# Gate weights of the first four experts in pages by row blocks, and one embedding piece in the seventh group

## The chip, the cores and the metric

The kernel runs on one core of a Trainium2 chip. The metric is the device time of one execution in microseconds (us); the times given are medians of several executions. Five engines work side by side: TensorE (PE; its weight loads are shown as PEld), VectorE (DVE), ScalarE (ACT), GpSimd (POOL) and SyncE (SP), which issues the transfers from the chip's memory (HBM). Sixteen DMA engines carry the transfers.

## The reference

One decoder layer over 256 tokens of width 1024, followed by a last RMSNorm. What is computed after the token mixer matters here:

```
h   = RMSNorm(x)
[z | xBC | dt | q | k | v | g_ssd | g_att] = h @ W_in
x   = x + (sigmoid(g_ssd) * SSD(...) @ W_ssd_out + sigmoid(g_att) * MoBA(...) @ W_att_out) @ W_o
x   = x + HierMoE(RMSNorm(x))            # 4 groups of 8 experts; top-1 group, top-2 experts in it
x   = x + sigmoid(RMSNorm(x) @ W_pg) * (p @ W_ple)
out = RMSNorm(x)
```

An expert has a gate and an up matrix of 1024 x 256 and a down matrix of 256 x 1024, float32: 1 MB each, so 96 MB for the 32 experts, all of which are read.

## The kernel before, in words

**The first part** (to about 285 us) is the input projection, the state-space mixer, the attention and the output projections. Each weight block is loaded, split into two parts by ACT and DVE (`w_split`), and multiplied on PE. The planner of the language orders the instructions of PE, ACT, DVE and POOL here by simulated costs; two stretches (`start`, `middle`) and the end (`ends`) are in the order in which they are written. SP's order is always the written one.

**Pages.** The pool `pgp` has 26 pages (NPAGE, line 45) of 8 KB in each of the 128 partitions. A 1 MB weight tile fills one. A page comes back when the last instruction that reads its tile is done; a load that needs a page waits for that on SP, and everything behind it on SP waits too. `prefetch(n)` (line 854) takes n entries from `queue` (line 846) and issues their loads. The entries are, for each group of four experts, four gate tiles, four up tiles, four down tiles. In the last group the up and down tiles are loaded in halves; before it stand the loads for the embedding (PLE_AT), and after it the four blocks of the last gate matrix (`pgr`). During the first part `prefetch` is called at fixed steps (PREFETCH, line 29); at the end of `middle` it is called until 25 entries have been issued (line 1193): both matrices of groups 0 and 1, their down tiles, and the first gate tile of group 2.

**The groups.** `quad(q)` (line 1278) does four experts: a gather of their tokens (`gather_quad`; group 0 is gathered in `middle`), the gate product, the up product (both into `pgu`, the loop over i at line 1286, over k at 1289 and over the four experts j at 1292), the weights of the combination (`combine_weights`), the activation (`hidden`), the down product (`down`, two halves n) and the scatter. After the gate product and after the up product the four tiles are dropped and up to four loads are issued (lines 1295 to 1297); after `down` four more (line 1309). In group 0 it is three and three, since two pages go to `hTg1` and `y_sb`.

**The embedding.** `embed()` (line 1398) is called before `quad(6)`. It spreads the last norm's weights, transposes p and returns `piece(t, c)` and `piece_out(t, c)`: two 128x512 products into one accumulator (PE), and its copy to SBUF on ACT. There are four pieces. `quad(7)` stands in the written order and calls two of them from `inside`, between the first and the second half of the up product; the third stands in `hidden`, and the fourth around `down(7, 0)`.

**The end** (lines 1555 to 1628): `down` of group 7, scatter, transposes, the last gate product (`ple_gate`, needs the `pgr` blocks), the last norm.

Accumulators: the tag `acc` has four PSUM banks, used in turn by gathers, downs, scatters and pieces.

Of the kernel before, what the change touches and what calls it, by code (L numbers as in the profile page):

```python
# [25 lines left out]
NK = D // P  # L26
# [12 lines left out]
EARLY_SPLITS = 5  # L39
SPLIT_FIRST = 260  # L40
PLE_AT = 72
EMBED_AT = 6
MAXOV = 16
EPS = 1e-6
NPAGE = 26
# [135 lines left out]
def emit(ctx, tc, nc, A, out):  # L181
    V, SC, PE, G, SP = nc.vector, nc.scalar, nc.tensor, nc.gpsimd, nc.sync
# [7 lines left out]
    def pg(shape, name, dt=F32):  # L190
        return pgp.tile([P] + shape, dt, tag="pg", name=name)

    def qt(shape, name, dt=F32):
        return qp.tile([P] + shape, dt, tag="qt", name=name)

    def acc(name, n=2):
        return [psp.tile([P, 512], F32, tag="acc", name=f"{name}_{i}", bufs=4) for i in range(n)]

    def ps1(shape, name, parts=P, dt=F32):
        return psp.tile([parts] + shape, dt, tag="s", name=name, bufs=2)  # L200
# [46 lines left out]
    def spread(row, ones, name):  # L247

        for c, o in enumerate(acc(name)):
            mm(o, ones, row[0:1, 512 * c:512 * c + 512], True, True)  # L250
            SC.copy(row[:, 512 * c:512 * c + 512], o)
# [554 lines left out]
        T["OT_hi"], T["OT_lo"] = OT_hi, OT_lo  # L806


    EW = {}
    PG_ORDER = [(0, 0), (0, 1), (1, 0), (1, 1)]  # L810
    pgraw, tail = [], {}
    nload = [0]
# [1 line left out]
    def expert_load(e, w):  # L814
        if w[0] == "d":
            if w != "d1":
                EW["d", e] = pg([4, 512], f"wd{e}")
            r = slice(2 * int(w[1]), 2 * int(w[1]) + 2) if w[1:] else slice(0, 4)
            SP.dma_start(EW["d", e][:, r], A["w_d"][e].rearrange("(p r) d -> p r d", r=4)[:, r])
        else:  # L820
            if w[1:] != "1":
                EW[w[0], e] = pg([NK, 256], f"w{w[0]}{e}")
            r = slice(4 * int(w[1]), 4 * int(w[1]) + 4) if w[1:] else slice(0, NK)
            SP.dma_start(EW[w[0], e][:, r], A["w_" + w[0]][e].rearrange("(p k) f -> p k f", k=NK)[:, r])

# [13 lines left out]
    def ple_gate_load(kh, c):  # L839
# [3 lines left out]
                             ap=[[2048, P], [1, 2048]]))  # L843
        pgraw.append(raw)

    queue = deque((expert_load, 4 * q + j, w) for q in range(NE // 4) for w in "gud" for j in range(4))
    for _ in range(8):
        queue.pop()
    queue.extend((expert_load, NE - 4 + j, w) for w in ("u0", "u1", "d0", "d1") for j in range(4))
# [4 lines left out]
    def prefetch(n):  # L854

        for _ in range(min(n, len(queue))):
            f, *a = queue.popleft()
            f(*a)
            nload[0] += 1
# [348 lines left out]
    def gather_quad(q):  # L1208
        if q == 1 or q % 2 == 0:
            hTg["page"] = pg([NK, 256], f"hTg{q}")  # L1210
        g, sel = hTg["page"][:, :, P * (q % 2):P * (q % 2) + P], new_sel(q)
        for t in range(NT):
            select(sel, q, t)
        gather(lambda a, b: g[:, a:b], lambda t: flat(sel, t), P, str(q), SC)
        hTg[q] = (lambda k: g[:, k]), sel
# [45 lines left out]
    def combine_weights(q, sel):  # L1261
        sq = qt([512], f"selw{q}")
        for t in range(NT):
            V.tensor_tensor(sq[:, t * P:(t + 1) * P].rearrange("p (e c) -> p e c", e=4), sel[:, t],
                            comb[:, t, 4 * q:4 * q + 4, None].to_broadcast([P, 4, CAP]), op=OP.mult)
        sw = weights_T(sq, sq[:, 256:512], P, str(q))
        return sw, factors(lambda t: flat(sel, t), P, str(q))

    def down(q, n, py, hT):
        for c in range(2):  # L1270
            for j in range(4):
                mm(py[n][32 * j:32 * j + 32, :], hT[:, c, 32 * j:32 * j + 32],
                   EW["d", 4 * q + j][:, 2 * n + c, :], c == 0, c == 1)
        if n:
            for j in range(4):
                EW.pop(("d", 4 * q + j))

    def quad(q, between=lambda: None, inside=lambda: None, wait=lambda: None):
        if q:
            gather_quad(q)  # L1280
        g, sel = hTg.pop(q)
        if q % 2:
            hTg.pop("page")
        es = range(4 * q, 4 * q + 4)
        pgu = ps1([512], f"gu{q}")
        for i, w in enumerate("gu"):
            if (q, i) == (7, 1):
                sw, f = combine_weights(q, sel)
            for k in range(NK):
                if (i, k) == (1, 4):  # L1290
                    inside()
                for j in range(4):
                    mm(pgu[32 * j:32 * j + 32, 256 * i:256 * i + 256], g(k)[:, 32 * j:32 * j + 32],
                       EW[w, 4 * q + j][:, k, :], k == 0, k == NK - 1)
            for j in range(4):
                EW.pop((w, 4 * q + j))
            prefetch(4 - (q == 0))
        if q == 0:
            hT0.clear()
        if q < 7:  # L1300
            sw, f = combine_weights(q, sel)
        g = None
        between()
        hT = hidden(pgu, f, P, str(q), wait=wait)
        if q == 7:
            return sw, hT
        py = acc(f"py{q}")
        down(q, 0, py, hT), down(q, 1, py, hT)
        prefetch(4)
        y = [qt([512], f"ye{q}{c}") for c in range(2)]  # L1310
        for c in range(2):
            (V.tensor_copy if c else SC.copy)(y[c], py[c])  # L1312
        scatter(sw, y, P, str(q))

    def load_rounds():
        return nc.values_load(nov_i, min_val=0, max_val=MAXOV - 1,
                              skip_runtime_bounds_check_because="512 choices fill at most 15 rounds beyond the first")
# [80 lines left out]
    def embed():  # L1398

        pin, wple, pT = tail["pin"], tail.pop("wple"), tail["pT"]  # L1400
        spread(tail["fnw"], pT[0:1, 0, 0:P], "fnw")
        ppt = ps2([2, S], "ppT")
        for k in range(2):
            for t in range(NT):
                PE.transpose(ppt[:, k, t * P:(t + 1) * P], pin[:, t, k * P:(k + 1) * P], ident)
        SC.copy(pT, ppt)
        pe = pe_[0] = pg([NT, D], "pemb")

        def piece(t, c, ks=(0, 1)):
            if (t, c) not in pps:  # L1410
                pps[t, c] = acc(f"pp{t}{c}", 1)[0]
            for k in ks:
                mm(pps[t, c], pT[:, k, t * P:(t + 1) * P], wple[:, k, half(c)], k == 0, k == 1)

        def piece_out(t, c):
            SC.activation(pe[:, t, half(c)], pps.pop((t, c)), AF.Copy, scale=0.5)

        return piece, piece_out

    for q in range(7):  # L1420
        if q == EMBED_AT:
            piece, piece_out = embed()
            nov = load_rounds()
        quad(q)
    while queue:
        prefetch(1)
    y_sb = ys[0]
# [120 lines left out]
                SC.activation(o, fin[t][:, 1, s], AF.Copy, scale=inv)  # L1548
            SP.dma_start(out[t * P:(t + 1) * P, s], o)

    def two_pieces():
        piece(0, 0), piece_out(0, 0)
        piece(0, 1), piece_out(0, 1)

    sw, hT = quad(7, other_rounds, two_pieces, lambda: piece(1, 0))
    piece_out(1, 0)
    py = acc("py7")
    y = [qt([512], f"ye7{c}") for c in range(2)]
# [5 lines left out]
    piece = None  # L1564
# [16 lines left out]
    hT = sw = y = py = None  # L1581
# [63 lines left out]
```

## Time and profile before

| | |
|---|---|
| median of 3 runs | 530.16 us (530.08 to 530.96) |
| profiled execution | 530.37 us, its span 528.6 us |
| PE busy | 495.0 us (94%) |
| DVE busy | 287.0 us (54%) |
| ACT busy | 212.8 us (40%) |
| DMA | 154.78 MB, 292 GB/s from HBM over the span |

The span is what the trace covers; 1.8 us of the execution lie outside it. A busy PE in this profile is one that has a matmul in it, also where that matmul runs at half clock. The busy share over the whole span mixes stages with different limits; which resource ends a stage last has to be read stage by stage.

### The profile page before, as it was taken

To read this page: it belongs to the slowest core of one execution; us is meant where nothing else is said; L and a number is where in the kernel's file an instruction comes from. 1 tells how busy PE (TensorE), PEld (TensorE's weight loads), DVE (VectorE), ACT (ScalarE), POOL (GpSimd) and SP (SyncE) were. 2 spreads that over 40 slices of the span, in tenths; PEclk is the share of its full clock that TensorE was granted. 3 is DMA by queue.
4 is the path that set the end of the run, shared out by engine and by line. 5 is a ranking of instruction groups with operands and counts; after the bars stand their busy time and mean duration, and the time that the engine had idled before them with its cause. 6 is when DMAs were issued, how large, how long until landed. Compare 5 with 4: busy or idle time off the path is not lost. (4 is left out here: it accounts for less than half of the span.)

```text
span 528.6 us, 9502 instructions
## 1 busy us (share of the span) xinstructions
PE 495.0 (94%) x3911; PEld 380.6 (72%) x3911; DVE 287.0 (54%) x585; ACT 212.8 (40%) x428; POOL 16.1 (3%) x22
## 2 busy tenths in 40 slices
PE   6999999999999999999999999898898989699993
PEld 3899887798889979899998855363554635254583
DVE  4899788886659497545585533033130312030675
ACT  5836759537456086544154321111101112012674
POOL 3000012000000000000000000000000000000001
PEclk9999999999999999999999999899989989899998
DMA  8990077365429204697969989999999999999802
GB/s 306 428 410 8 1 249 318 112 221 227 172 81 387 79 2 160 249 392 255 367 233 383 400 329 427 426 428 426 426 425 425 425 423 427 426 420 417 343 1 79
DMA packets 29842, 154.78 MB, mean 293 GB/s; under 512 B 4307, under 2 KB 9187, under 8 KB 14437
## 3 DMA queue, kind: packets, MB, share of 16 engines
q1 hardware_dynamic: 29796, 154.15, 72.4%
q8 instruction: 31, 0.51, 0.4%
q14 instruction: 15, 0.11, 0.1%
HBM read 153.08 MB, written 1.06 MB: 292 GB/s over the span
## 5 line engine op out<-in xcount | busy, mean ns | idle before, releaser
L293 DVE TENSOR_TENSOR wl<-wr,wh 128x1024 fp32r<-128x1024 f32 (+4 forms) x92 | 100.7, 1131 | 9.7 <-ACT wh L292 8.8
L292 ACT CAST wh<-wr 128x1024 fp32r<-128x1024 f32 (+4 forms) x92 | 82.6, 961 | 14.4 <-DMA wr<-in_w_ao 4.3
L208 PE MATMUL py<-wd,hq 128*32 128x512 f32 x256 | 39.2, 711 | 3.2 <-ACT hq L1237 3.2
L208 PE MATMUL ps_t<-wl,hT_hi 128*128 128x448 f32 (+2 forms) x112 | 39.9, 374 | 1.6 <-DVE wl L293 1.5
L208 PE MATMUL ps_t<-wh,hT_hi 128*128 128x448 f32 (+2 forms) x112 | 39.5, 375 | 0.0
L208 PE MATMUL ps_t<-wh,hT_lo 128*128 128x448 f32 (+2 forms) x112 | 39.1, 367 | 0.0
L1230 DVE SCALAR_TENSOR_TENSOR hq<-hq,gu 128x256 f32<-128x256 f32 x8 | 3.4, 421 | 61.7 <-ACT hq L1229 61.7
L208 PE MATMUL gu<-wu,hTg 128*32 128x256 f32 x512 | 32.8, 396 | 3.2 <-DMA wu<-in_w_u 3.2
L208 PE MATMUL gat<-sel,x_sb 128*128 128x128 f32 x256 | 30.4, 276 | 0.5 <-DVE ng L1066 0.5
L208 PEld LDWEIGHTS gat<-sel,x_sb 128*128 128x128 f32 x256 | 29.4, 192 | 1.8 <-issue 1.2
L208 PE MATMUL sca<-ye,selw 128*128 128x512 f32 x64 | 30.1, 611 | 0.1
L208 PE MATMUL gu<-wg,hTg 128*32 128x256 f32 x512 | 30.1, 381 | 0.0
L208 PEld LDWEIGHTS gu<-wu,hTg 128*32 128x32 f32 x512 | 17.5, 114 | 16.7 <-DMA wu<-in_w_u 4.2
L208 PEld LDWEIGHTS py<-wd,hq 128*32 128x32 f32 x256 | 10.4, 125 | 26.2 <-issue 18.8
L1312 DVE COPY ye<-py 128x512 f32<-128x512 f32 x7 | 4.8, 691 | 41.8 <-PE py L208 41.8
L208 PEld LDWEIGHTS ps_t<-wl,hT_hi 128*128 128x128 f32 x112 | 21.0, 191 | 5.1 <-DVE wl L293 3.6
L208 PEld LDWEIGHTS sca<-ye,selw 128*128 128x128 f32 x64 | 11.0, 189 | 18.0 <-issue 10.1
L208 PEld LDWEIGHTS ps_t<-wh,hT_lo 128*128 128x128 f32 x112 | 21.3, 190 | 1.8 <-DVE hT_lo L358 0.4
L208 PEld LDWEIGHTS gu<-wg,hTg 128*32 128x32 f32 x512 | 15.4, 110 | 9.9 <-issue 0.2
L1229 ACT ACTIVATE hq<-gu,f 128x256 f32<-128x256 f32 x8 | 3.8, 473 | 46.5 <-PE gu L208 45.0
L208 PEld LDWEIGHTS ps_t<-wh,hT_hi 128*128 128x128 f32 x112 | 21.2, 192 | 1.7
L1136 ACT ACTIVATE hTg<-gat,par 128x128 f32<-128x128 f32 x32 | 9.2, 368 | 28.2 <-PE gat L208 26.8
(310 smaller groups left out, 1095.3 us busy)
## 6 DMA issues: line engine op xcount, KB each, us to landing
wg<-in_w_g SPq DMA_DIRECT2D x32, 1024.0 KB, 13.3
wu<-in_w_u SPq DMA_DIRECT2D x28, 1024.0 KB, 15.9
wd<-in_w_d SPq DMA_DIRECT2D x28, 1024.0 KB, 19.4
wr<-in_w_in SPq DMA_DIRECT2D x16, 1024.0 KB, 5.4
wr<-in_w_in SPq DMA_DIRECT2D x10, 896.0 KB, 10.1
wr<-in_w_so SPq DMA_DIRECT2D x4, 1024.0 KB, 4.8
wr<-in_w_ao SPq DMA_DIRECT2D x4, 1024.0 KB, 7.1
wr<-in_w_o SPq DMA_DIRECT2D x4, 1024.0 KB, 6.8
```

Source lines behind the costliest of these rows:

```text
L208: mm = lambda o, l, r, start, stop: PE.matmul(o, l, r, start=start, stop=stop, skip_group_check=True)
L292: SC.copy(hi[:, s], raw[:, s])
L293: V.tensor_tensor(lo[:, s], raw[:, s], hi[:, s].bitcast(F32), op=OP.subtract)
L1136: SC.activation(dst(k + i, k + i + 1)[:, 0], o[:, i], AF.Copy, scale=R("mnw")[:, k + i:k + i + 1])
L1229: SC.activation(hd[0:n], pgu[:, 0:256], AF.Tanh, scale=f[0:n, 0:1])
L1230: V.scalar_tensor_tensor(hd[0:n], hd[0:n], 1.0, pgu[:, 0:256], op0=OP.add, op1=OP.mult)
L1312: (V.tensor_copy if c else SC.copy)(y[c], py[c])
```

## The change

The gate tiles of experts 0 to 3 are no longer one page for each expert. Page i (i = 0 to 3, `first_load`) holds the row blocks k = 2i and 2i + 1 of all four experts; it is filled by four transfers of 256 KB, one for each expert, with 2 KB for each partition. The gate product of group 0 reads those pages; after each odd k one page is dropped and one load is issued. After its up product two loads are issued instead of three. The count of entries and their order behind the first four are the same. The second edit: the first of the four embedding pieces is written behind `quad(6)` instead of inside `quad(7)`.

```
+    def first_load(i):
+
+        FW[i] = pg([4, 2, 256], f"wf{i}")
+        for j in range(4):
+            SP.dma_start(FW[i][:, j], A["w_g"][j].rearrange("(p k) f -> p k f", k=NK)[:, 2 * i:2 * i + 2])
+
     queue = deque((expert_load, 4 * q + j, w) for q in range(NE // 4) for w in "gud" for j in range(4))
+    for _ in range(4):
+        queue.popleft()
+    queue.extendleft((first_load, 3 - i) for i in range(4))
...
                     mm(pgu[32 * j:32 * j + 32, 256 * i:256 * i + 256], g(k)[:, 32 * j:32 * j + 32],
-                       EW[w, 4 * q + j][:, k, :], k == 0, k == NK - 1)
-            for j in range(4):
-                EW.pop((w, 4 * q + j))
-            prefetch(4 - (q == 0))
+                       FW[k // 2][:, j, k % 2] if (q, i) == (0, 0) else EW[w, 4 * q + j][:, k, :], k == 0, k == NK - 1)
+                if (q, i, k % 2) == (0, 0, 1):
+                    FW.pop(k // 2)
+                    prefetch(1)
+            if (q, i) != (0, 0):
+                for j in range(4):
+                    EW.pop((w, 4 * q + j))
+                prefetch(2 if q == 0 else 4)
...
-    for q in range(7):
-        if q == EMBED_AT:
-            piece, piece_out = embed()
-            nov = load_rounds()
+    for q in range(6):
         quad(q)
+    piece, piece_out = embed()
+    nov = load_rounds()
+    quad(6)
+    piece(0, 0), piece_out(0, 0)
...
-    def two_pieces():
-        piece(0, 0), piece_out(0, 0)
+    def one_piece():
         piece(0, 1), piece_out(0, 1)
 
-    sw, hT = quad(7, other_rounds, two_pieces, lambda: piece(1, 0))
+    sw, hT = quad(7, other_rounds, one_piece, lambda: piece(1, 0))
```

## Rows read from the trace of the kernel before

**Rows 1.** The page's 40 equal slices of the span (13.2 us each): PE busy in tenths, the DMA engines' busy share in tenths, and GB/s.

```profile
PE   6999999999999999999999999898898989699993
...
DMA  8990077365429204697969989999999999999802
GB/s 306 428 410 8 1 249 318 112 221 227 172 81 387 79 2 160 249 392 255 367 233 383 400 329 427 426 428 426 426 425 425 425 423 427 426 420 417 343 1 79
```

**Rows 2.** Busy time by stretch, around group 0's gate product and after it: start and end, length, then busy us (and instructions) of PE, PEld, DVE, ACT, POOL, the granted clock, the DMA share and GB/s.

```profile
307.00:307.50 0.50, 0.50 (x18) 0.28 (x11) 0.46 (x3) 0.00 (x0) 0.00 (x0) 1.00 0.63 246
307.50:308.00 0.50, 0.50 (x16) 0.33 (x12) 0.37 (x2) 0.00 (x0) 0.00 (x0) 1.00 0.31 131
308.00:308.50 0.50, 0.50 (x16) 0.30 (x12) 0.00 (x0) 0.00 (x0) 0.00 (x0) 1.00 0.20 82
308.50:309.00 0.50, 0.50 (x18) 0.27 (x10) 0.00 (x0) 0.00 (x0) 0.00 (x0) 1.00 0.27 115
309.00:309.50 0.50, 0.50 (x16) 0.33 (x12) 0.00 (x0) 0.00 (x0) 0.00 (x0) 1.00 0.08 33
309.50:310.00 0.50, 0.50 (x16) 0.31 (x12) 0.00 (x0) 0.00 (x0) 0.00 (x0) 1.00 0.54 98
310.00:310.50 0.50, 0.50 (x17) 0.26 (x8) 0.00 (x0) 0.00 (x0) 0.00 (x0) 1.00 0.60 98
310.50:311.00 0.50, 0.50 (x16) 0.33 (x12) 0.00 (x0) 0.00 (x0) 0.00 (x0) 1.00 0.64 147
311.00:311.50 0.50, 0.50 (x16) 0.32 (x12) 0.00 (x0) 0.00 (x0) 0.00 (x0) 1.00 1.02 426
311.50:332.80 21.30, 20.10 (x182) 11.16 (x174) 6.59 (x17) 3.32 (x9) 0.00 (x0) 0.92 1.01 425
```

**Rows 3.** The timeline of SP's queue: start us, length us, the load, how many in a row (the last length includes waits between them).

```profile
298.51 0.42 SPq L824 DMA_DIRECT2D wg<-in_w_g  x1
...
308.97 1.28 SPq L824 DMA_DIRECT2D wg<-in_w_g  x3
310.34 3.37 SPq L824 DMA_DIRECT2D wu<-in_w_u  x4
313.79 0.38 SPq L819 DMA_DIRECT2D wd<-in_w_d  x1
...
321.22 11.87 SPq L819 DMA_DIRECT2D wd<-in_w_d  x3
...
332.76 0.33 SPq L819 DMA_DIRECT2D wd<-in_w_d  x1
```

**Rows 4.** The timeline of PE in groups 0 and 1: start us, length us, the product, how many instructions (a float32 product is two), and the idle time before it with what ended it.

```profile
305.30 3.66 PE L208 MATMUL gu<-wg,hTg 128*32 128x256 f32 x64
...
330.82 1.93 PE L208 MATMUL gu<-wg,hTg 128*32 128x256 f32 x32
332.57 3.64 PE L208 MATMUL gu<-wu,hTg 128*32 128x256 f32 x64
```

**Rows 5.** The gate load that SP issued at 298.5, and from its issue to its landing.

```profile
L824 SPq DMA_DIRECT2D wg<-in_w_g x1: 422/422/422, 298.5 to 298.5; - x1
...
DMA to landing us min/median/max: 11.2/11.2/11.2
```

**Rows 6.** The timeline of PE in group 6 (its up and down products) and in group 7 (its up and down products with the pieces); columns as in rows 4.

```profile
447.67 0.60 PE L208 MATMUL gu<-wu,hTg 128*32 128x256 f32 x4
449.70 0.62 PE L208 MATMUL gu<-wu,hTg 128*32 128x256 f32 x2 [1.42 <-DMA wu<-in_w_u]
452.13 5.33 PE L208 MATMUL gu<-wu,hTg 128*32 128x256 f32 x58 [1.81 <-DMA wu<-in_w_u]
459.14 0.41 PE L1235 MATMUL hdT<-ident,hq 128*128 128x128 f32 x2 [1.69 <-DVE hq L1231]
460.01 5.54 PE L208 MATMUL py<-wd,hq 128*32 128x512 f32 x32 [0.46 <-ACT hq L1237]
...
476.99 1.93 PE L208 MATMUL gu<-wu,hTg 128*32 128x256 f32 x32
478.86 3.70 PE L208 MATMUL pp<-wple,rows 128*128 128x512 f32 x8
482.49 1.93 PE L208 MATMUL gu<-wu,hTg 128*32 128x256 f32 x32
...
487.71 1.92 PE L208 MATMUL py<-wd,hq 128*32 128x512 f32 x16
...
492.92 1.92 PE L208 MATMUL py<-wd,hq 128*32 128x512 f32 x16
```

**Rows 7.** A weight load of PE in group 6's down product, from the timeline, and the transfer that it waited for.

```profile
461.94 0.16 PEld L208 LDWEIGHTS py<-wd,hq 128*32 128x32 f32 x8 [0.91 <-DMA wd<-in_w_d]
```

**Rows 8.** The last half load of group 7's up tiles, its landing, and the fourth and the last half load of its down tiles.

```profile
L824 SPq DMA_DIRECT2D wu<-in_w_u x1: 328/328/328, 471.9 to 471.9; - x1
...
DMA to landing us min/median/max: 10.0/10.0/10.0
...
L819 SPq DMA_DIRECT2D wd<-in_w_d x1: 327/327/327, 476.8 to 476.8; - x1
...
L819 SPq DMA_DIRECT2D wd<-in_w_d x1: 328/328/328, 481.8 to 481.8; - x1
```

**Rows 9.** Busy time by stretch (columns as in rows 2): the last stretch with a lower granted clock before the end, and all that follows.

```profile
452.56:455.97 3.41, 3.41 (x36) 1.74 (x32) 0.00 (x0) 0.00 (x0) 0.00 (x0) 0.50 1.01 425
455.97:524.20 68.23, 62.04 (x424) 37.97 (x416) 32.26 (x61) 27.85 (x56) 2.71 (x4) 1.00 0.65 270
```

**Rows 10.** SP's queue where the first gate tiles are loaded, ACT's casts of the weight blocks that follow, and busy time by stretch there (columns as in rows 2).

```profile
156.74 4.70 SPq L824 DMA_DIRECT2D wg<-in_w_g  x4
164.00 0.33 SPq L275 DMA_DIRECT2D wr<-in_w_in  x1
...
189.32 1.99 ACT L292 CAST wh<-wr 128x1024 fp32r<-128x1024 f32 x2
...
170.00:189.00 19.00, 18.59 (x156) 17.64 (x154) 10.27 (x21) 4.21 (x12) 1.02 (x1) 1.00 0.25 94
```

**Rows 11.** Busy time by stretch where whole tiles (8 KB for each partition) and where half tiles (4 KB) are loaded; columns as in rows 2.

```profile
344.00:428.00 84.00, 75.70 (x803) 43.13 (x802) 23.83 (x51) 11.19 (x31) 0.19 (x1) 0.98 1.01 425
...
470.00:486.00 16.00, 15.67 (x170) 9.23 (x169) 2.16 (x6) 3.18 (x8) 0.00 (x0) 1.00 1.03 419
```

More of the change, by code (lines that the diff above doesn't have):

```diff
@@ L41 @@
 PLE_AT = 72
-EMBED_AT = 6
 MAXOV = 16
@@ L806, in attention @@
         T["OT_hi"], T["OT_lo"] = OT_hi, OT_lo
-    EW = {}
+    EW, FW = {}, {}
     PG_ORDER = [(0, 0), (0, 1), (1, 0), (1, 1)]
```

## The prediction

> **What bounds the kernel now.** I read the page's slices first [rows 1]. PE shows 8 or 9 tenths almost everywhere, so the share alone doesn't name a limit. The DMA row does: up to slice 24 it swings between nothing and full, and from slice 25 to 37 (317 to 489 us) it stands at 9 with 417 to 428 GB/s. A stretch that moves bytes at one constant rate for 170 us is limited by that rate if somebody waits for the bytes. The timeline of PE shows who does, and where: up to group 5 hardly a product waits for a load, but in group 6 the up product stops at 449.70 and 452.13 for up tiles, together 3.2 us of idle PE [rows 6], and the down product stops until 461.94 for a down tile [rows 7]. From 461.94 on PE goes through the down product, the scatter, the gather, the gate product and group 7 without another wait for a load worth naming, and everything up to the end hangs on it. So the end of the kernel is set by when the down tiles of group 6 land, that is by how early the stream of loads has been, plus the PE work behind 461.94.
>
> How early the stream is, is decided where it last had a gap. Rows 2 show it: the DMA share falls to 0.31 at 307.5 us, to 0.08 at 309.0, and is back at 1.02 at 311.0. Measured against 425 GB/s the nine half microseconds from 307.0 to 311.5 lack 2.9 us of transfer (sum of (425 - GB/s)/425 x 0.5). The reason stands in rows 3: after the load at 298.51 the next is issued at 308.97, when the gate product of group 0, which runs from 305.30 [rows 4], is done and gives four pages back at once.
>
> **The change part by part.**
>
> *Pages one by one.* The product takes 3.66 us [rows 4], so a pair of k is done every 0.9 us: pages come at about 306.2, 307.1, 308.0 and 309.0 instead of four at 309.0. PE's 64 instructions are the same, with the same columns. SP gets four waits instead of one; behind them on SP stand only the loads of groups 2 to 7, which gain from it. The first load can be issued 2.7 us earlier. What follows is less than that, for two reasons.
>
> First, the queues don't all run dry at once. A share of 0.31, 0.20 and 0.27 from 307.5 to 309.0 is four or five of sixteen engines still at the load of 298.5, which landed 11.2 us later, at 309.7 [rows 5]. For these the gap is only from about 309.5 to the restart at 311.0, 1.5 us. The Trainium skill (DMA: Bandwidth & Descriptors, "Why a DMA increments its semaphore by 16 and not by 1") says that a transfer's engines finish independently and that only the full count means that all has landed. By that rule what counts for a waiting product is the slowest engine, and the most that this step could give would be 1.5 us; by the mean of the engines it would be 2.9 us.
>
> Second, and this decides: the stream next depends on a page return at 332.76 us [rows 3], when the gate product of group 1 ends (it began its second half at 330.82 and the up product follows at 332.57 [rows 4]). That gate product still returns four pages at once, it isn't earlier, since PE does not wait for loads here, and before it no page is free: ten loads are issued from 308.97 to 321.22 [rows 3], 10.49 MB. From 309.5 to 332.8 the engines move 0.17 MB up to 311.0, 0.21 MB up to 311.5 and 21.3 us x 425 GB/s = 9.05 MB after that [rows 2], 9.43 MB in all. So at 332.8 there are 1.06 MB left, 2.5 us of transfer. A restart isn't free: after the issue at 308.97 the full rate came at 311.0, 2.0 us later, and until then 0.19 MB came (33 to 147 GB/s), worth 0.4 us; so a restart costs 1.6 us from the issue. If the stream is ahead by more than 2.5 - 1.6 = 0.9 us, it falls dry at 332.8 and loses the rest. If the ramp is cheaper the second time (no row shows another such restart), it keeps up to 2.0 us: nothing can come in the first 0.5 us after an issue [rows 2]. I take 0.9, by the only restart measured. Further on a load lands 10 us or more after its issue [rows 8], so a stream that is 0.9 us ahead meets no third gap. All loads up to the last then land 0.9 us earlier, and so do the waits of group 6 and the point 461.94.
>
> *The first loads.* Four loads at 156.74 to 161.44 become sixteen. SP needs some 0.4 us for an issue (1.28 us for three [rows 3]), so up to 5 us more; behind them stands the weight block issued at 164.00. The next cast of a block is at 189.32, and between 170 and 189 us the DMA share is 0.25 [rows 10]: the block lands well before. The 4 MB move in runs of 2 KB instead of 8 KB. Runs of 4 KB went at 419 GB/s against 425 [rows 11]; another halving costs, as an estimate from these, 0.1 to 0.3 us on 9.9, in a stretch with idle engines. I cost both at nothing. If that cover were gone, it would be 5 us at most, before group 0.
>
> *The piece.* In group 7 two pieces stand between the halves of the up product, 478.86 to 482.49: 3.63 us, 1.8 each [rows 6]. The last half tile of that product is issued at 471.86 and lands 10.0 us later, at 481.9 [rows 8]. So 3.0 us of the pieces cover a wait and 0.6 us are on the path. With one piece PE is at the second half at 480.7 and waits until 481.9: the gain is 0.6 us, not 1.8. What is late next: the fourth half of the down tiles, issued at 476.8, some 10 us to land, 486.8, against 487.71, and the last one, issued at 481.8, against 492.92 [rows 6, 8]; with 0.9 and 1.1 us of slack neither takes the 0.6 back. The moved piece is four PE instructions and one ACT copy of 0.6 us; no load, and nothing on SP or POOL. In group 6 PE idles 3.2 us for up tiles and 1.69 us before the transpose [rows 6], so the planner has room for it; if it puts it behind the scatter instead, it is 1.8 us on PE's path, which equals what leaves group 7, and the gain is 0. Bounds 0 and 0.6; I take 0.6, because the holes are in reach and ACT waits there too.
>
> *Sum.* 0.9 + 0.6 = 1.5 us off the span of 528.6, so 527.1, and 528.9 with the 1.8 us outside it. The profiled execution is 0.2 us above the median of 530.16, so for a median I say 528.7.
>
> **Rivals.**
>
> *The second gap doesn't open*, because the ramp at 332.8 is cheap or the slow engines decide and are still fed. For it: 2.5 us of loads are still queued. Against: the restart in rows 2. The stream keeps 1.5 (slowest engines) to 2.9 us (all), say 2.3: 530.2 - 2.3 - 0.6 = 527.3.
>
> *The stream gains, the piece doesn't* (it stands on the path in group 6): 530.2 - 0.9 = 529.3.
>
> *The change doesn't do what it says*: the early pages buy nothing at 461.94, because the engines that are late at 309.5 stay the late ones, and only the piece counts, or nothing: 529.6 to 530.2.
>
> *Slower: TensorE's clock.* It is at 0.50, that is 1.2 GHz, from 452.56 for 3.41 us [rows 9]; before that PE had little to do (the wait for a load from 450.3 to 452.13 [rows 6]). This stretch lies ahead of 461.94, and the wait for the down tile hides it now; from 455.97 to the end the clock is 1.00. The change moves the waits of group 6 and opens one of 1.2 us in group 7. If a low stretch then falls into the work behind 461.94, it costs up to 1.7 us (3.41/2), two of them 3.4. From the point that more than the 1.5 us gained goes, the kernel is slower: two give 530.2 - 1.5 + 3.4 = 532.1. Against: the moved piece fills one of the waits. The Trainium skill (TensorE: Matmul & The Clock Gate, "HAM oscillation — how this bites in real kernels") tells the same of products that wait for loads, that the clock falls and the next burst starts slow; the rows of group 6 agree.
>
> **How the numbers follow.** Forecast 528.7, chance 0.42, its own range 528.0 to 529.4. No second gap 0.17; the piece on the path 0.14; nothing of the stream 0.12; the clock 0.15. A difference of 0.2%, 1.06 us, is about what a measurement can tell from none. Faster by that, under 529.1: 0.34 of the forecast's 0.42 and all of the first rival, 0.51. Within it: the other 0.08, 0.14 and 0.12, 0.34. Slower: 0.15. The range for 8 in 10 goes from 526.9 (the first rival with its upper bounds) to 530.6 and leaves out most of the clock's case.
>
> **What would show it.** Pages: SP issues gate loads at about 306.3, 307.2, 308.1 and 309.0, and the share between 307 and 311 stays above 0.6. Second gap: from 333 to 335 us the share, now full, falls below 1; if it stays at 1, the first rival is right. Stream: the down product of group 6 goes on at about 461.0 instead of 461.94. Piece: four `pp` instructions before group 7's gather instead of none, four instead of eight between the halves, and an idle PE in front of the second half that ends with a load. Clock: a 0.50 after 456 us. I am wrong at the root if group 0's gate product starts later than 305.3, for then the order of the first part has changed.

## The result and the profile after

| | before | after |
|---|---|---|
| median of 20 runs each, side by side (us) | 530.80 | 535.39 |
| lowest to highest | 529.71 to 534.88 | 532.71 to 538.99 |
| profiled execution: time, span | 530.37, 528.6 | 535.24, 533.4 |
| mean granted clock of that execution | 0.980 | 0.975 |

The ratio is 1.0079, with a 95% interval from 1.0056 to 1.0101. The change makes the kernel slower by 0.8%, some 4.2 us by the ratio and 4.6 by the medians; 528.7 was forecast, with 526.9 to 530.6 as the range. Runs of one kernel scatter by 5 to 6 us here, so one profile shows where a step goes, and medians what it is worth.

The loads first. The timeline of SP's queue after the change (columns as in [rows 3]):

```profile
301.22 10.08 SPq L823 DMA_DIRECT2D wg<-in_w_g  x4
311.72 4.68 SPq L823 DMA_DIRECT2D wu<-in_w_u  x4
316.49 19.30 SPq L818 DMA_DIRECT2D wd<-in_w_d  x4
...
335.46 0.33 SPq L818 DMA_DIRECT2D wd<-in_w_d  x1
```

The load of 298.51 is now at 301.22, so everything here is 2.7 us late. Behind it the pages do come back one by one: the row of four gate loads lasts 10.08 us because each waits for its own page (issued at 301.22, 309.13, 309.99 and 310.86), and the up load follows at 311.72. Busy time by stretch after the change, at both gaps (columns as in [rows 2]):

```profile
309.50:310.00 0.50, 0.50 (x16) 0.30 (x12) 0.47 (x3) 0.00 (x0) 0.00 (x0) 1.00 0.66 279
...
310.50:311.00 0.50, 0.50 (x16) 0.29 (x12) 0.10 (x1) 0.00 (x0) 0.00 (x0) 1.00 0.70 197
...
334.00:335.00 1.00, 1.00 (x24) 0.63 (x20) 0.00 (x0) 0.00 (x0) 0.00 (x0) 1.00 1.01 426
335.00:336.00 1.00, 1.00 (x28) 0.60 (x20) 0.00 (x0) 0.00 (x0) 0.00 (x0) 1.00 0.55 221
336.00:337.00 1.00, 1.00 (x25) 0.57 (x21) 0.00 (x0) 0.00 (x0) 0.00 (x0) 1.00 0.92 164
337.00:338.00 1.00, 1.00 (x24) 0.65 (x20) 0.00 (x0) 0.00 (x0) 0.00 (x0) 1.00 0.62 262
```

The gap of [rows 2], where the share fell to 0.08, is now a dip: the lowest half microsecond still moves 197 GB/s. And a second gap has opened at the return of group 1's pages, where the page is free at 335.46: the three microseconds from 335 move 221, 164 and 262 GB/s, against 425 that is a loss of ((425 - 221) + (425 - 164) + (425 - 262)) / 425 = 1.5 us. Before, the stream was full up to this return (332.76 us) [rows 2] and behind it, in its own trace:

```profile
330.00:334.00 4.00, 4.00 (x74) 2.37 (x70) 0.00 (x0) 0.00 (x0) 0.00 (x0) 1.00 1.02 426
334.00:335.00 1.00, 1.00 (x28) 0.57 (x20) 0.00 (x0) 0.00 (x0) 0.00 (x0) 1.00 1.01 426
```

Now PE from the scatter of group 6 on, its timeline after the change (columns as in [rows 4]):

```profile
471.31 1.88 PE L207 MATMUL pp<-wple,rows 128*128 128x512 f32 x4
...
482.86 1.98 PE L207 MATMUL pp<-wple,rows 128*128 128x512 f32 x4
484.77 0.63 PE L207 MATMUL gu<-wu,hTg 128*32 128x256 f32 x4
485.73 1.96 PE L207 MATMUL pp<-wple,rows 128*128 128x512 f32 x4 [0.33 <-ACTq L1334]
487.62 1.92 PE L207 MATMUL gu<-wu,hTg 128*32 128x256 f32 x28
491.22 0.41 PE L1243 MATMUL hdT<-ident,hq 128*128 128x128 f32 x2 [1.69 <-DVE hq L1239]
```

The moved piece (471.31) stands alone between scatter and gather, on PE's path. In group 7 one piece is gone from between the halves of the up product, but the planner has cut the second half: four instructions, then the branch and the next piece (485.73), then the other 28. Before, that half was one row of 32 [rows 6] with the third piece behind it:

```profile
484.75 1.96 PE L208 MATMUL pp<-wple,rows 128*128 128x512 f32 x4 [0.33 <-PEq L1322]
486.54 0.38 PE L1235 MATMUL hdT<-ident,hq 128*128 128x128 f32 x2
```

The piece covered the chain from the product to the transpose `hdT`, which had no wait of its own; now `hdT` waits 1.69 us for `hq`. So the description of the kernel ("`quad(7)` stands in the written order") does not hold for PE here: the 28 instructions run behind the branch and the piece, though they are written ahead of both.

Last, the first part. The timeline of PE after the change, where the products of the gate `ga` begin (only rows that waited are shown):

```profile
188.83 0.87 PE L207 MATMUL o<-e,qkv 128*64 128x256 f32 x8 [0.57 <-ACT e L776]
...
190.37 0.89 PE L207 MATMUL sc<-rT,rT 64*128 64x128 f32 x6 [0.67 <-DVE xsT L697]
...
191.61 0.39 PE L207 MATMUL ps_ga<-hT_hi,wh 128*128 128x256 f32 x1 [0.34 <-ACT wh L291]
...
192.88 0.58 PE L207 MATMUL ps_ga<-hT_hi,wl 128*128 128x256 f32 x1 [0.77 <-DVE wl L292]
```

The same products before the change:

```profile
188.98 0.87 PE L208 MATMUL o<-e,qkv 128*64 128x256 f32 x8 [0.41 <-ACT e L777]
189.78 0.92 PE L208 MATMUL sc<-rT,rT 64*128 64x128 f32 x6
190.63 0.39 PE L208 MATMUL ps_ga<-hT_hi,wh 128*128 128x256 f32 x1
...
191.68 0.39 PE L208 MATMUL ps_ga<-hT_hi,wl 128*128 128x256 f32 x1 [0.54 <-DVE wl L293]
```

Before, PE idles 0.41 + 0.54 = 0.95 us there; after, 0.57 + 0.67 + 0.34 + 0.77 = 2.35. Then the clock falls. Busy time by stretch, after (columns as in [rows 2]):

```profile
189.47:192.88 3.41, 1.63 (x14) 0.81 (x8) 3.41 (x6) 3.41 (x7) 0.00 (x0) 1.00 0.01 2
192.88:196.29 3.41, 3.41 (x16) 3.41 (x17) 3.41 (x12) 3.41 (x6) 0.00 (x0) 0.50 0.00 0
```

From 192.88 on PE is busy all the time, at the granted clock 0.50, that is 1.2 GHz, for 3.41 us; before the change the clock is at 1.00 there. Nothing of the change is in this place: neither a page of the experts nor a piece.

So that no run's late start counts, the profiles are compared by stretches between the same PE instructions: from the first product of `gs` (160.21 before) to group 0's first product (305.30), from there to the second half of group 6's down product (462.39), from there to group 7's transpose (486.54), and on to the end of the span (528.57). In us, the change against before:

| profile | 160 to 305 | 305 to 462 | 462 to 487 | 487 to end |
|---|---|---|---|---|
| before, length | 145.09 | 157.09 | 24.15 | 42.03 |
| after | +3.02 | -0.41 | +2.39 | +0.19 |

The stream's stretch is the only one with a gain; two others lose 5.4 us. The experiments take them one at a time; their table stands behind them.

### The profile page after: what moved, and what is told of

It reads as the page before. It is cut to its first block, busy times and chain, and to the rows that moved or that the text cites. A ratio compares the mean times of both kernels' runs of the same rounds, so it can differ in the third digit from the quotient of the medians.

```text
span 533.4 us, 9511 instructions
## 1 busy us (share of the span) xinstructions
PE 496.1 (93%) x3911; PEld 381.2 (71%) x3911; DVE 286.8 (54%) x585; ACT 213.0 (40%) x428; POOL 16.5 (3%) x22
## 5 line engine op out<-in xcount | busy, mean ns | idle before, releaser
L207 PE MATMUL py<-wd,hq 128*32 128x512 f32 x256 | 36.7, 682 | 3.2 <-ACT hq L1245 3.2
L207 PE MATMUL gu<-wu,hTg 128*32 128x256 f32 x512 | 34.9, 402 | 3.8 <-DMA wu<-in_w_u 3.8
L207 PE MATMUL gu<-wg,hTg 128*32 128x256 f32 x448 | 26.5, 382 | 0.0
L207 PEld LDWEIGHTS gu<-wg,hTg 128*32 128x32 f32 x448 | 13.5, 110 | 8.7 <-issue 0.2
L207 PE MATMUL pso<-wh,mT 128*128 128x512 f32 (+1 forms) x64 | 18.8, 368 | 0.0
```

The lines of the kernel that those rows point to most:

```text
L207: mm = lambda o, l, r, start, stop: PE.matmul(o, l, r, start=start, stop=stop, skip_group_check=True)
```

## The experiments

Each was timed twelve times (`split` six) beside runs of the kernel before. The cuts of code are against the kernel before, in `one` and `two` against the kernel after; `...` marks what is left out. My theory at the start was: what costs is not the pages, but the order that the planner makes of sixteen loads in the first part, and a piece that stands on PE's path; the rivals were a low clock that falls there by chance, and the page layout itself.

**The layout alone** (`layout`). After's pages and sixteen loads, pieces as before. The product drops its four tiles at the end, as before:

```diff
+            if (q, i) == (0, 0):
+                for j in range(4):
+                    FW.pop(j)
+            else:
+                for j in range(4):
+                    EW.pop((w, 4 * q + j))
-            for j in range(4):
-                EW.pop((w, 4 * q + j))
             prefetch(4 - (q == 0))
```

> Only the page layout with its sixteen loads; the four pages are still given back at once, and the pieces stay where they were. My theory (the sixteen loads change the planner's order of the first part, and that costs some 2.7 us before group 0's first product): the product starts at about 308.0 instead of 305.3, the load behind it is issued at about 311.7, and the time is 2.2 to 3.0 us over that of before, since nothing of the gap is won back. Rival (the first part is late because of a low clock that came by chance, not by the order): the order differs but the product starts at 305 to 306, and the time is within 1 us of before. Second rival (the early return of pages, not the layout, is what costs): the time equals that of before.

Measured: 532.91 us, ratio 1.0035 [1.0012, 1.0058], that is 2.5 us over before by the medians and 1.9 by the ratio. The first stretch is 3.03 us longer, as in the whole change. One expectation missed: the loads behind the product went at 309.21, 310.07, 310.94 and 311.80, not together at 311.7. SP waits for each page's own last reader, so here row blocks came back one by one although the program drops them together.

**The whole change without the piece** (`pages`).

```diff
+                if (q, i, k % 2) == (0, 0, 1):
+                    FW.pop(k // 2)
+                    prefetch(1)
```

> The whole change without the piece: layout, sixteen loads, pages given back one by one. By my theory the product starts at 308.0, as with the layout alone, the loads behind it go at 309.1 to 311.7, and the gap at the return of group 1's pages (about 335.5) takes back all but some 0.9 us of what the early pages bring: 1.5 to 2.5 us over before, 0 to 0.9 less than the layout alone. Rival (the early pages bring 2 us or more): equal to before within 0.7 us. Rival (they bring nothing): the same as the layout alone.

Measured: 532.25 us, ratio 1.0020 [0.9995, 1.0045]; the interval holds 1, so by the times alone it isn't told apart from before. By what was just said this is the run with the layout alone once more, and the instructions of all engines come in the same order. Yet its first stretch is only 1.54 us longer. Busy time by stretch in `pages`:

```profile
189.47:192.88 3.41, 2.25 (x17) 1.49 (x16) 3.29 (x9) 2.00 (x4) 0.00 (x0) 1.00 0.00 0
192.88:196.29 3.41, 2.22 (x15) 1.64 (x15) 3.41 (x10) 3.41 (x6) 0.00 (x0) 1.00 0.01 2
196.29:199.70 3.41, 3.41 (x27) 3.02 (x27) 3.41 (x6) 3.41 (x5) 0.00 (x0) 1.00 0.00 0
```

This execution is 2.6 us later here: the product at 192.88 in `after` is this one, with the same wait.

```profile
195.47 0.39 PE L207 MATMUL ps_ga<-hT_hi,wl 128*128 128x256 f32 x1 [0.77 <-DVE wl L292]
```

The clock stays at 1.00 ahead of that product and behind it, where it fell in `after` and in `layout` (0.50 from 193.19 to 196.61 us). So the 3.0 us are two things: 1.5 us for the order, in all four profiles that have it (`after`, `layout`, `pages` and `split` below), and 1.5 us more in an execution in which the clock falls. The rival that the clock explains it all is wrong, and so is the theory that the order alone does.

The second gap, too, is not there in this profile. The page return is at 334.88, and around it:

```profile
335.00:336.00 1.00, 1.00 (x27) 0.57 (x23) 0.00 (x0) 0.00 (x0) 0.00 (x0) 1.00 1.03 426
336.00:337.00 1.00, 1.00 (x24) 0.63 (x20) 0.00 (x0) 0.00 (x0) 0.00 (x0) 1.00 0.97 385
```

In `after` a half-clock stretch of 3.41 us falls between the gate products of groups 0 and 1, from 319.17 (before the change, from 316.03), and the pages of group 1 come back 27.5 us behind group 0's first product (308.00 to 335.46). Here the clock is at 1.00 up to 341.47, and they come back after 25.8 us (309.11 to 334.88), before the stream has run dry.

**Sixteen loads and nothing else** (`split`), and **eight loads** (`split2`). Tiles and pages of before; only the loads of the first four experts' gate weights are cut:

```diff
+            if e < 4 and w == "g":
+                for i in range(4):
+                    r = slice(2 * i, 2 * i + 2)
+                    SP.dma_start(EW["g", e][:, r], ...)
+                return
```

with `range(2)` and slices of four rows in `split2`. By the order of the instructions of PE, DVE, ACT and POOL in the traces, `split` equals the whole change in the first part, and `split2` equals before.

> The pages of before, given back as before, but the first four gate weights come in sixteen loads (four row quarters for each expert), which gives the planner's order of the whole change in the first part and nothing else of it. My theory (what costs is the order that the planner makes of sixteen loads): the products of the gate ga wait for the casts of their weight block as in the run with the layout alone, group 0's first product starts 1.5 to 3.0 us later than with the order of before (3.0 where a half-clock stretch follows at about 193 us, 1.5 where it doesn't), the first gap stays as it is, and the time is 1.5 to 3.2 us over before. Rival (the page layout, that is strided tiles read by the product, is what costs): equal to before within 0.5 us.

> As the run with sixteen loads, but eight (two halves for each expert), which leaves the planner's order on all engines as in before. My theory: within 0.5 us of before, group 0's first product at 305 less or more the scatter of a start. Rival (more loads delay the weight blocks behind them on SP, whatever the order): 0.7 to 1.5 us over before, half of what sixteen cost.

Measured: `split` 532.70 us, ratio 1.0050 [1.0030, 1.0069]; `split2` 531.30 us, ratio 1.0003 [0.9982, 1.0024]. The first stretch: +1.53 and -0.01 us. (The ratio of `split` says 2.7 us, from 1.6 to 3.7: more than its profile, as it would be if the clock falls in some of its other executions, which no trace shows.) So it is not the layout. It is the order that comes with sixteen loads, and half as many cost nothing: in the rows that follow PE, ACT and DVE wait for one another, and between 157 and 200 us none of the three waits for a load. Sixteen loads under the order of before were not run. The timeline of ACT shows the first swap, before the change:

```profile
167.27 2.00 ACT L292 CAST wh<-wr 128x1024 fp32r<-128x1024 f32 x2 [3.50 <-PE ps_gs L208]
169.18 0.40 ACT L765 ACTIVATE e<-e,nm 128x128 f32<-128x128 f32 x1
```

and in `split`:

```profile
167.42 0.40 ACT L765 ACTIVATE e<-e,nm 128x128 f32<-128x128 f32 x1 [3.48 <-DVE nm L760]
...
169.19 1.98 ACT L292 CAST wh<-wr 128x1024 fp32r<-128x1024 f32 x2
```

The planner now puts the attention's exponentials ahead of the cast of a weight block, and the cast comes 1.9 us later, 0.2 of which is the later start of that execution. With it come the block's second half `wl`, the chain `sr`, `ssqc`, `xsT` on DVE (`sr` starts at 177.82 instead of 176.09), and the casts of the next block, for which PE then waits as seen above, in `split` too:

```profile
189.31 0.87 PE L208 MATMUL o<-e,qkv 128*64 128x256 f32 x8 [0.57 <-ACT e L777]
...
190.86 0.89 PE L208 MATMUL sc<-rT,rT 64*128 64x128 f32 x6 [0.68 <-DVE xsT L698]
...
192.09 0.38 PE L208 MATMUL ps_ga<-hT_hi,wh 128*128 128x256 f32 x1 [0.34 <-ACT wh L292]
...
193.37 0.39 PE L208 MATMUL ps_ga<-hT_hi,wl 128*128 128x256 f32 x1 [0.78 <-DVE wl L293]
```

The idle time is 0.57 + 0.68 + 0.34 + 0.78 = 2.37 us, 1.4 more than before, nearly all of the lost 1.5. Why the planner swaps just these two is not in a trace and stays open.

**The piece alone** (`piece`). Loads and pages of before:

```diff
-    for q in range(7):
-        if q == EMBED_AT:
...
+    quad(6)
+    piece(0, 0), piece_out(0, 0)
...
     def two_pieces():
-        piece(0, 0), piece_out(0, 0)
```

> Only the piece is moved; loads and pages as before. My theory: the piece stands on PE's path behind group 6's scatter (1.7 us), and group 7 gets back less than that, since the second half of its up product is now split by the other piece and the branch and no longer covers the chain that makes the transposed hidden tile: 1.5 to 2.5 us over before, group 0's first product at 305.3 as before, the transpose of group 7 waiting about 1.7 us. Rival (the piece only changes places, what it costs in group 6 leaves group 7): within 0.5 us of before. The prediction's step would be 0.6 us under before.

Measured: 532.66 us, ratio 1.0042 [1.0019, 1.0065]. The stretch from 462 to 487 is 2.39 us longer, as in the whole change, the others are equal within 0.02. The timeline of PE in `piece`:

```profile
468.60 1.88 PE L208 MATMUL pp<-wple,rows 128*128 128x512 f32 x4
...
483.02 1.96 PE L208 MATMUL pp<-wple,rows 128*128 128x512 f32 x4 [0.33 <-ACTq L1322]
484.91 1.92 PE L208 MATMUL gu<-wu,hTg 128*32 128x256 f32 x28
...
488.51 0.41 PE L1235 MATMUL hdT<-ident,hq 128*128 128x128 f32 x2 [1.69 <-DVE hq L1231]
```

Between scatter and gather, which begins at 470.32, it costs 470.32 - 468.60 = 1.72 us; the other 2.39 - 1.72 = 0.67 us are lost in group 7.

**The piece hidden in group 6** (`hid`). The same piece, in a hook ahead of group 6's transpose:

```diff
-        quad(q)
+            quad(6, wait=lambda: (piece(0, 0), piece_out(0, 0)))
+        else:
+            quad(q)
```

> The piece moved to group 6, but by hand in front of the transpose of its hidden tile, where PE idled 1.7 us, instead of behind the scatter; loads and pages as before. My theory: the 1.7 us in group 6 are hidden, and what is left is the loss in group 7, where the other piece and the branch split the second half of the up product: 0.3 to 1.0 us over before. Rival (it is the place in group 6 alone that costs, group 7 gives its 0.6 us back): 0.3 to 0.6 under before. Second rival (the place doesn't matter, PE has no room in group 6): 1.7 to 2.5 over before, as with the piece behind the scatter.

Measured: 531.55 us, ratio 1.0032 [1.0010, 1.0053]. The median is 0.9 us over that of before, the ratio says 1.7, with an interval from 0.5 to 2.8, so the size is only roughly known. The profile is clear: the stretch to 462 is 0.14 us shorter, the stretch from 462 to 487 is 0.73 us longer. Group 6 hides the piece, though not where the hook stands: PE runs it ahead of the gate product, at 443.06, and later waits for up tiles cover it. Group 7 alone loses. Its timeline of PE:

```profile
480.98 0.63 PE L208 MATMUL gu<-wu,hTg 128*32 128x256 f32 x4
482.00 1.95 PE L208 MATMUL pp<-wple,rows 128*128 128x512 f32 x4 [0.39 <-ACTq L1322]
483.88 1.92 PE L208 MATMUL gu<-wu,hTg 128*32 128x256 f32 x28
487.49 0.41 PE L1235 MATMUL hdT<-ident,hq 128*128 128x128 f32 x2 [1.69 <-DVE hq L1231]
```

The 28 instructions at 483.88 wait for no load: the last half tile landed at 482.05. What stands in their way is the branch and the piece.

**One load for each page** (`one`, run again as `one_again`). After's pages and their return, but each page comes in one load of 1 MB, so that the first part keeps the order of before:

```diff
-        for j in range(4):
-            SP.dma_start(FW[i][:, j], ...)
+        SP.dma_start(FW[i].rearrange("p j k f -> p j (k f)"),
+                     A["w_g"][0:4].rearrange("j (p a k) f -> p j a (k f)", a=4, k=2)[:, :, i])
```

> Pages by row blocks and given back one by one, but one load of 1 MB for each page instead of four of 256 KB, so that the order of the first part stays that of before; pieces as before. My theory: group 0's first product starts at 305.3 as before, the loads behind it go at 306.3 to 309.0, a gap opens at 332.8 and takes back part, and the time is 0.3 to 1.2 us under before. Rival (no gap at 332.8): 1.5 to 2.9 us under before. Rival (row blocks as such are slow, because their runs are shorter): the product of group 0 waits for its pages and the time is above that of before.

> The run with one load for each page once more, beside the two others of this set: 1.1 to 2.1 us under before, as the first time (1.63). If it is within 0.5 us of before, the gain of the first time was scatter.

Measured: 528.82 us, ratio 0.9969 [0.9948, 0.9989], and 530.27 us, ratio 0.9975 [0.9953, 0.9997]. Both are faster than before; by the ratios 1.6 and 1.3 us, by the medians 1.6 and 0.8. The first is more than the 0.3 to 1.2 that I expected, the second by its median less than the 1.1 to 2.1. The first stretch is +0.00 and +0.01 us. A second gap opens here too. Busy time by stretch in `one`:

```profile
332.00:333.00 1.00, 1.00 (x28) 0.57 (x23) 0.00 (x0) 0.00 (x0) 0.00 (x0) 1.00 0.54 213
333.00:334.00 1.00, 1.00 (x24) 0.62 (x20) 0.00 (x0) 0.00 (x0) 0.00 (x0) 1.00 0.81 188
```

It loses (212 + 237) / 425 = 1.1 us in these two. The two profiles differ: to 462 `one` gains 2.26 us, `one_again` 0.16. Part of it is in the stream: behind the second gap `one_again` falls to 279, 205 and 344 GB/s in the three microseconds from 336, where `one` moves 418 to 434, and that is 1.0 us. Why, no trace shows. What `one` gains, it doesn't keep: its stretch to 487 is 0.91 us longer, because group 7's gate product takes 3.96 us where it took 3.66, and the first half of its up product 2.54 where it took 1.93 [rows 6], its half tiles being the next that are late.

**Two groups in row blocks** (`two`). As `one`, with group 1's gate weights in the same pages:

```diff
+    for q in range(2):
+        for i in range(4):
+            queue[12 * q + i] = (first_load, q, i)
```

> The gate weights of the first eight experts by row blocks, one load for each page, so that group 1's pages too come back one by one; order of the first part and pieces as before. My theory: loads are issued from about 329.5 on instead of 332.1, the second gap (in the run with one load for a page it costs some 1.2 us of transfer between 330 and 335) closes, and the time is 2.2 to 3.5 us under before, 0.6 to 1.5 under that run. Rival (the second gap costs nothing behind 449 us, because PE and not the stream sets the end there): the same as that run, 1.6 under before.

Measured: 529.00 us, ratio 0.9969 [0.9952, 0.9985], the same as `one`. The pages of group 1 did come back one by one, from 331.36, and the stream kept 369 and 385 GB/s from 332 to 336, a loss of some 0.5 us instead of 1.1; but to 462 the profile gains 1.34 us, about the mean of `one` and `one_again` (1.21). The smaller second gap brought nothing that can be measured, against my expectation of 0.6 to 1.5 us under `one`. Whether that is because something else ends there, or because group 1's product itself was 1.3 us later in this execution (a half-clock stretch of 6.83 us from 314.95), can't be told apart by it.

**The whole change with one load for each page** (`one_piece`). After, with the loads of `one`.

> The whole change, the moved piece too, but one load of 1 MB for each page instead of four, so that the first part keeps the order of before. My theory: the parts add up, about 1.6 us from the pages under before and 2.2 us from the piece over it: 0.2 to 1.2 us over before, some 3.6 under the whole change, group 0's first product at 305 as in before. Rival (the sixteen loads or their order are not what made the whole change slow): 3 us or more over before.

Measured: 532.12 us, ratio 1.0025 [1.0003, 1.0047]: 1.0 us over before by the medians, 1.3 by the ratio. The parts add up: -1.5 for the pages and +2.2 for the piece would be +0.7. The change from sixteen loads to four alone makes it 1.0025 instead of 1.0079. As in `pages`, no half-clock stretch falls between the first two gate products of this profile (the next is at 337.72), the pages come back after 25.8 us, at 330.92, and the stream moves 401 GB/s from 331 to 335.

**Another piece** (`one_h10`). As `one`, and the piece that stood behind group 7's up product goes to group 6:

```diff
+            quad(6, wait=lambda: piece(1, 0))
+            piece_out(1, 0)
...
-    sw, hT = quad(7, other_rounds, two_pieces, lambda: piece(1, 0))
-    piece_out(1, 0)
+    sw, hT = quad(7, other_rounds, two_pieces)
```

> Pages with one load each, and another piece is moved: the one that stood between group 7's up product and the transpose of its hidden tile goes to group 6, where the planner puts it ahead of the gate product, before the waits for up tiles; the two in the middle of group 7's up product stay. My theory: in group 6 it is hidden by the waits for the up tiles, in group 7 the second half of the up product stays whole ahead of the branch, and the transpose waits only for the chain behind that product, some 1.75 us as in the run with the piece hidden in group 6: 0.2 to 0.6 us under the run with one load for each page, 1.8 to 2.4 under before. Rival (group 6 has no free time on PE): 1 us or more over that run.

Measured: 529.65 us, ratio 0.9967 [0.9945, 0.9988]; beside `one_again` at 530.27 in the same set that is 0.6 us less by the medians and 0.4 by the ratios, as expected and within the scatter. Under before it is 1.4 us by the medians and 1.8 by the ratio, where 1.8 to 2.4 was expected. Its timeline of PE:

```profile
442.74 1.88 PE L207 MATMUL pp<-wple,rows 128*128 128x512 f32 x4
...
483.35 1.93 PE L207 MATMUL gu<-wu,hTg 128*32 128x256 f32 x32
486.99 0.41 PE L1243 MATMUL hdT<-ident,hq 128*128 128x128 f32 x2 [1.71 <-DVE hq L1239]
```

The piece goes ahead of group 6's gate product (442.74), where later waits for up tiles cover it, and the second half in group 7 is whole again. This is the fastest of the versions by its ratio; it isn't told apart from `one`. In this profile the clock's case came true. Busy time by stretch:

```profile
462.26:465.67 3.41, 3.41 (x11) 0.71 (x4) 0.00 (x0) 0.59 (x1) 0.00 (x0) 0.50 1.01 428
```

A half-clock stretch lies behind the wait for the down tile, and the stretch from 462 to 487 is 1.28 us longer: 1.70 for the clock (3.41 / 2; twenty instructions of the down product take 5.32 us here and 3.62 in `hid`), less the 0.4 of the moved piece.

All profiles by stretches, in us against before (145.09, 157.09, 24.15, 42.03), with the ratio of the times of their sets:

| profile | 160 to 305 | 305 to 462 | 462 to 487 | 487 to end | ratio of the times |
|---|---|---|---|---|---|
| after | +3.02 | -0.41 | +2.39 | +0.19 | 1.0079 |
| layout | +3.03 | -1.63 | +0.55 | +0.19 | 1.0035 |
| pages | +1.54 | -1.43 | -0.01 | +0.26 | 1.0020 |
| split | +1.53 | -0.05 | 0.00 | +0.24 | 1.0050 |
| split2 | -0.01 | -0.13 | 0.00 | +0.53 | 1.0003 |
| piece | 0.00 | +0.02 | +2.39 | -0.02 | 1.0042 |
| hid | 0.00 | -0.14 | +0.73 | 0.00 | 1.0032 |
| one | 0.00 | -2.26 | +0.91 | -0.05 | 0.9969 |
| one_again | +0.01 | -0.16 | +0.67 | -0.04 | 0.9975 |
| two | +0.01 | -1.34 | 0.00 | 0.00 | 0.9969 |
| one_piece | 0.00 | -2.08 | +2.39 | -0.01 | 1.0025 |
| one_h10 | -0.01 | -0.68 | +1.28 | -0.02 | 0.9967 |

## Why the prediction was wrong

**The step that failed most was the first loads.** The prediction costed the sixteen loads at nothing, because SP has time and the block behind them lands well before its cast, and it gave 5 us as the price if that cover were gone. That argument was about the transfer, and the transfer was indeed hidden: `split2` with twice the loads of before costs nothing, and with sixteen no engine waits for a load there. But the order of ACT, DVE and PE in this part is not written out; the planner makes it for each program, and sixteen loads gave it another order between 167 and 200 us, which costs 1.5 us and in two of its four profiles 1.5 us more by the clock. The prediction named the sign by which to see this (group 0's gate product later than 305.3; it starts at 308.00) and gave it neither a price nor a chance. As an absolute time the sign is loose: in `split2`, with the order of before, that product starts at 306.23, because the whole execution began later. The changed order should have been a rival on the slower side.

**The piece was the second.** "The planner has room for it" in group 6 was right about the room (`hid` and `one_h10` hide it there) and wrong about what the planner does: the piece went behind the scatter, 1.72 us on the path, which was the lower bound's case. And the bound itself was too kind. It set 1.8 us lost against 1.8 gained, "the gain is 0". Group 7 gives nothing back: with one piece less the branch and the next piece, which had covered the chain to the transpose, run in the middle of the up product. My reading is that the planner fills an expected wait for the last half tile with them; why it does so is not shown. So it is +2.39 us in the profile (2.2 by the medians of `piece`) where -0.6 was forecast; 1.72 + 0.67 in place of 0 + (-0.6).

**The pages were right in the main.** One by one they come, the first gap shrinks to a dip, and in `after`, `layout`, `one`, `one_again` and `one_h10` the second gap opens at the return of group 1's pages, as worked out from the restart in [rows 2]. It costs 1.5 us in `after` and 1.1 in `one`. In `pages` and `one_piece` it does not open. The prediction took the return as fixed ("it isn't earlier, since PE does not wait for loads here"), but it comes 1.7 us earlier where no half-clock stretch falls ahead of it; so in two profiles the first rival came true, for a reason that it did not name. The mean rate of the 40 us from group 0's first product shows what the stream keeps: 394 GB/s before, 399 in `after`, 408 in `one`, 387 in `one_again`, 417 in `pages` and in `one_piece`. The gain at 462 does not follow these rates (`one` 2.26 us, `pages` 1.43), so what releases the late tiles of group 6 is not settled. The forecast had the stream keep 0.9 us, and the runs without the other two effects keep 1.3 to 1.6 by their ratios, some 0.5 us more.

**The clock** as a rival behind 461.94 was drawn right in its price (1.7 us a stretch, seen in `one_h10`), but in the profile of the whole change it struck elsewhere: at 192.88, 1.5 us. The half-clock stretch of `after` in group 6 lies at 452.29 and is 6.83 us long; the stretch to 462 is still shorter than before.

By the terms: forecast -0.9 for the stream, 0 for the loads and -0.6 for the piece, that is -1.5. Measured by parts, -1.5 for the pages, +1.5 for the order, about +1.5 for the clock where it falls, and +2.2 for the piece, that is +2.2 to +3.7; the whole change measures +4.2, with an interval from 3.0 to 5.4. What is left between 3.7 and 4.2 is within the scatter of the parts. By the ratios alone, which mix executions with and without the fall of the clock, the parts are +2.7 (`split`), -1.5 and +2.2, that is +3.4, inside the interval. The range of the forecast missed it because both errors lay on one side and neither had a case on the slower side. (Its lower end has a small slip: the first rival with its upper bounds gives 530.2 - 2.9 - 0.6 = 526.7, not 526.9. Nothing hangs on it.)

## What to carry to other kernels

Where a planner orders the engines, count an edit's instructions as a change of the whole order, not only by their own time: compare the two orders first, and when a far stretch has moved, the cheap remedy is to keep the number of instructions (one strided load in place of four turned 0.8% slower into 0.25% slower, and without the piece into 0.3% faster). A piece of work that "covers a wait" is covering whatever the planner puts next to it, so price its removal by the chain that it will uncover. Bytes moved early in one place can be lost again at the next page return, as in `after` and `one`, and whether they are can hang on when PE gets there; look for that place before counting them.

## What was not expected of the hardware

The granted clock fell in `after` (at 192.88) and `layout` (at 193.19) and stayed up in `pages` and `split`, with the same order of instructions and the same idle times of PE (2.35 to 2.37 us in four waits, the longest 0.78). In the nine profiles with the order of before it never fell there. `layout` and `pages` run the same instructions in the same order on PE, DVE, ACT and POOL, and one lost 1.5 us there and the other not; what decides it, these runs do not show. The Trainium skill (TensorE: Matmul & The Clock Gate, "HAM oscillation — how this bites in real kernels") tells of products that wait for loads; here no load was waited for, only work of ACT and DVE.

A single profile of the stream is worth less than I took it for: `one` and `one_again` are the same kernel, and to 462 us they differ by 2.1 us.
